# Two-layer decoder trunk, one core: probabilities of pairs 0 to 4 scaled on ScalarE, transposed through DRAM

## The chip, the cores and the metric

The kernel runs on one core of a Trainium2 chip. The metric is the device time of one execution, in microseconds; the figure given is the median of three runs. The core's engines each work through an instruction queue of their own, in order: TensorE (PE; its weight loads are listed as PEld), VectorE (DVE), ScalarE (ACT), GpSimd (POOL) and SyncE (SP), which here only starts transfers.

## The reference

Two decoder layers over 256 tokens of width 1024, 16 heads of 64, float32 throughout. Layer 0 uses forgetting attention: causal softmax, with a bias from the cumulated logarithms of forget gates. Layer 1 uses block-sparse attention, whose one block holds all 256 tokens, so that it is causal softmax with a relative-position bias. Each layer goes on with a gated feed-forward part and a gated embedding.

```python
u = _rmsnorm(h, attn_norm_g[i])
proj = u @ w_in                         # q, k, v (and forget gates in layer 0)
logits = einsum('bhqd,bhkd->bhqk', q, k) * HEAD_DIM ** -0.5 + bias   # -inf above the diagonal
probs = softmax(logits)
o = einsum('bhqk,bhkd->bhqd', probs, v)
h = h + merge_heads(o) @ w_o
u = _rmsnorm(h, ffn_norm_g[i])
gu = u @ ffn_w_in[i]
h = h + (silu(gu[..., :D_FF]) * gu[..., D_FF:]) @ ffn_w_out[i]
gate = sigmoid(_rmsnorm(h, ple_norm_g[i]) @ ple_w_gate[i])
h = h + gate * (p[i] @ ple_w_up[i])
```

At the end stands a last `_rmsnorm`.

## The kernel before

Activations lie with features on the 128 partitions and the 256 tokens along the free axis. Weights stream in chunks of 512 KB on SP's queue into `raw` (six buffers). ScalarE rounds each chunk to the reduced type fp32r (`whi`, L163 and L181), VectorE takes the remainder (`wlo`, L165 and L182), six buffers each, and `mm3` multiplies in three matmuls (L91 to L93): high by high, high by low, low by high. The same split into a high and a low part, `split` (L284 on ScalarE, L285 on VectorE), is made of q and k and of the attention's output.

Attention works on eight pairs of heads (NP = 8). For a pair j:

- `project(j, 0)` and `project(j, 1)`: 48 matmuls into the bank `pq`. VectorE scales the result (`qkt`, L498), then `qkh` and `qkl` are its two parts.
- `scores`: TensorE writes the logits of each head to `sp` (three products L514, and one L511 of the first 128 queries with the first 128 keys; in layer 0 the bias by L371). VectorE adds the mask or bias and takes the extreme of each row (`e`, `mn`, L528; an instruction of 128 columns and one of 256 for each head). ScalarE takes the exponentials and their sums (L532), VectorE the reciprocals of the sums (`rc`, L535), and VectorE multiplies `e` by them (L538, two instructions, for 2 x 128 and 2 x 256 columns).
- `transposes`: six TensorE transposes a pair (L551) put the probabilities' keys on the partitions, in a bank `pp`; ScalarE copies each head's 384 columns out (`pt`, L556).
- `values`: eight instructions of TensorE a pair, with v and `pt`, into `po` (L565 and L567), and a split into the two parts of `o`.

The loop takes two pairs at a time: project pairs j and j+1, then transposes and values of pairs whose probabilities are ready, then the scores of pairs j-1 and j. In its last turn stand the transposes of pairs 3 and 4, values of pairs 1, 2 and 3, the scores of 5 and 6, and those of 7 (their end is `end`). Behind it follow the output weights: `wo(hf, c)` multiplies pairs 2c and 2c+1 into half hf of the output, (0,0) and (1,0) first; between them lie the transposes of pairs 5 to 7 and the values of pairs 4 to 7.

A scheduler sets the order of instructions on each engine from the order in the program; `tc.issue_after(ins)` places what is written inside it behind an instruction. The tiles `e` have four buffers, `pt` four, `fp` four.

At the very end `by_token` turns the output from features to tokens: VectorE transposes blocks of 32 x 32 (L765), two transfers on SP's queue write the result to DRAM (`dh`, L768), and eight read it back in another order (`ut`, L770).

## Time and profile before

| what | value |
|---|---|
| median of three runs | 646.74 us (646.62 to 647.48) |
| profiled execution | 646.52 us |
| its span, first to last instruction | 644.7 us |
| granted TensorE clock | 0.998 |
| TensorE busy | 636.2 us (99%) |
| VectorE busy | 456.0 us (71%) |
| ScalarE busy | 373.7 us (58%) |
| GpSimd busy | 9.9 us (2%) |

All instruction times below are of the profiled execution, counted from the start of its span. The attention of layer 0 lies at about 30 to 105 us, that of layer 1 at 345 to 420 us. A profile row of a group reads: line, engine, operation, output and inputs, shapes and count; then busy time in us and mean of one in ns; then idle time ahead of them and what ended it. A row of a timeline reads: start, duration, engine, line, operation, count, and in brackets idle time ahead of it and what ended it. An arrow names the engine and instruction that was waited for. Neighbouring instructions of one engine overlap by about 0.1 us, so they start at a shorter pitch than their durations.

### The profile page before, as it was taken

The page shows a single profiled execution, that of the slowest core. Times are in us where ns is not written, and L with a number is a line of the kernel's source. Part 1 is how long each engine was busy: PE and PEld are TensorE (multiplying, and loading weights), DVE is VectorE, ACT ScalarE, POOL GpSimd, SP SyncE. Part 2 cuts the span into 40 slices and gives each one's busy share as a digit, 9 for nine tenths or more (in the row PEclk, how much of TensorE's full clock was granted, in tenths as well). Part 3 has the DMA queues.
Part 4 walks back from the last instruction along what each step waited for, and adds up shares of the span by engine and source line. Part 5 has one row for each costly group of instructions (what it writes and reads, how often), then busy time and mean ns, then how long its engine had stood idle before and what let it go on. Part 6 is the DMA issues. An engine that isn't in the chain of part 4 may idle for free.

```text
span 644.7 us, 13185 instructions
## 1 busy us (share of the span) xinstructions
PE 636.2 (99%) x5357; PEld 615.2 (95%) x5357; DVE 456.0 (71%) x734; ACT 373.7 (58%) x633; POOL 9.9 (2%) x23
## 2 busy tenths in 40 slices
PE   9999999999999999999999999999999999999995
PEld 7899999999999999999989999999999999999984
DVE  7789875786666666668895888677666666666685
ACT  6786685754444445448665677666444444454653
POOL 0100000000000000000000000000000000000001
PEclk9999999999999999999999999999999999999999
DMA  8865544397766666666577554436766666666523
GB/s 341 309 207 183 152 132 156 99 348 264 247 199 192 195 192 214 189 205 196 191 245 273 179 173 138 130 102 202 227 199 197 198 197 190 193 205 192 192 97 100
DMA packets 37533, 126.33 MB, mean 196 GB/s; under 512 B 4096, under 2 KB 7776, under 8 KB 37472
## 3 DMA queue, kind: packets, MB, share of 16 engines
q1 hardware_dynamic: 37040, 124.87, 60.7%
q8 instruction: 42, 0.69, 0.4%
q10 hardware_dynamic: 432, 0.62, 0.3%
q14 instruction: 19, 0.16, 0.1%
HBM read 123.35 MB, written 5.27 MB: 200 GB/s over the span
## 4 chain that ended last, share of the span: by engine, by line
PE 96%; issue 2%; DMA 1%; DVE 0%; POOL 0%; POOLq 0%; DVEq 0%; ACT 0%
PE gu L91 12%; PE gu L92 12%; PE gu L93 12%; PE fo L93 6%; PE fo L91 6%; PE fo L92 6%; PE pq L91 5%; PE pq L93 5%; PE pq L92 5%; PE v L422 4%; PE wo L91 2%; PE wo L93 2%; PE wo L92 2%; PE pp L551 2%; PE pg L91 2%
## 5 line engine op out<-in xcount | busy, mean ns | idle before, releaser
L165 DVE TENSOR_TENSOR wlo<-raw,whi 128x1024 fp32r<-128x1024 f32 (+1 forms) x166 | 201.0, 1217 | 84.9 <-ACT whi L163 79.2
L163 ACT ACTIVATE whi<-raw 128x1024 fp32r<-128x1024 f32 x164 | 172.5, 1059 | 120.9 <-issue 53.7
L91 PE MATMUL gu<-g,whi 128*128 128x256 f32 x704 | 194.9, 277 | 0.0
L92 PE MATMUL gu<-g,whi 128*128 128x256 f32 x704 | 194.7, 277 | 0.0
L93 PE MATMUL gu<-g,wlo 128*128 128x256 f32 x704 | 194.5, 276 | 0.0
L93 PEld LDWEIGHTS gu<-g,wlo 128*128 128x128 f32 x704 | 132.2, 188 | 0.0
L92 PEld LDWEIGHTS gu<-g,whi 128*128 128x128 f32 x704 | 132.2, 188 | 0.1
L91 PEld LDWEIGHTS gu<-g,whi 128*128 128x128 f32 x704 | 132.2, 188 | 0.0
L93 PE MATMUL fo<-fp,wlo 128*128 128x256 f32 x352 | 97.4, 277 | 0.0
L91 PE MATMUL fo<-fp,whi 128*128 128x256 f32 x352 | 97.3, 276 | 0.0
L92 PE MATMUL fo<-fp,whi 128*128 128x256 f32 x352 | 97.3, 276 | 0.0
L182 DVE TENSOR_TENSOR wlo<-raw,whi 128x1080 fp32r<-128x1080 f32 x44 | 56.4, 1282 | 41.9 <-ACT whi L181 41.3
L91 PE MATMUL pq<-g,whi 128*128 128x256 f32 x256 | 71.3, 279 | 0.0
L181 ACT ACTIVATE whi<-raw 128x1080 fp32r<-128x1080 f32 x44 | 48.5, 1103 | 38.9 <-PE gu L92 27.1
L93 PE MATMUL pq<-g,wlo 128*128 128x256 f32 x256 | 70.8, 277 | 0.0
L92 PE MATMUL pq<-g,whi 128*128 128x256 f32 x256 | 70.8, 276 | 0.0
L92 PEld LDWEIGHTS fo<-fp,whi 128*128 128x128 f32 x352 | 66.2, 188 | 0.0
L91 PEld LDWEIGHTS fo<-fp,whi 128*128 128x128 f32 x352 | 66.1, 188 | 0.0
L93 PEld LDWEIGHTS fo<-fp,wlo 128*128 128x128 f32 x352 | 66.1, 188 | 0.0
L91 PEld LDWEIGHTS pq<-g,whi 128*128 128x128 f32 x256 | 48.1, 188 | 0.6 <-issue 0.2
L92 PEld LDWEIGHTS pq<-g,whi 128*128 128x128 f32 x256 | 48.1, 188 | 0.1
L93 PEld LDWEIGHTS pq<-g,wlo 128*128 128x128 f32 x256 | 48.1, 188 | 0.0
(184 smaller groups left out, 983.1 us busy)
## 6 DMA issues: line engine op xcount, KB each, us to landing
raw<-w SPq DMA_DIRECT2D x169, 512.0 KB, 4.2
raw<-w SPq DMA_DIRECT2D x44, 540.0 KB, 4.4
d<-d SPq DMA_DIRECT2D x4, 768.0 KB, 7.1
bias<-d SPq DMA_DIRECT2D x4, 512.0 KB, 7.0
dh<-end SPq DMA_DIRECT2D x2, 512.0 KB, 2.6
ut<-dh SPq DMA_DIRECT2D x8, 128.0 KB, 3.0
hw<-wx SPq DMA_DIRECT2D x1, 640.0 KB, 6.5
hw<-xr SPq DMA_DIRECT2D x1, 640.0 KB, 7.8
```

What stands on the lines that cost most here:

```text
L91: mm(o, ah, bh, start=start, stop=False, skip_group_check=True)
L92: mm(o, ah, bl, start=False, stop=False, skip_group_check=True)
L93: return mm(o, al, bh, start=False, stop=stop, skip_group_check=True)
L163: state["hi"] = state[f"hi{i}"] = nc.scalar.activation(hi[:, c], raw[:, c], AF.Copy)
L165: nc.vector.tensor_tensor(lo[:, c], raw[:, c], f32(hi[:, c]), op=ALU.subtract)
L181: nc.scalar.activation(ht, raw[:, 0:WW], AF.Copy)
L182: nc.vector.tensor_tensor(lt, raw[:, 0:WW], f32(ht), op=ALU.subtract)
L422: got = mm(bks[2 * t + hf], x[a][:, t * P:(t + 1) * P], w[b][:, hf * HC:(hf + 1) * HC], start=k + a + b == 0, stop=k + b == KT, skip_group ...
L551: got = nc.tensor.transpose(pp[:, q * P:(q + 1) * P], e[:, s, q * P:(q + 1) * P], ident)
```

## The change

For pairs 0 to 4 of both layers (TURNED = 5):

- VectorE's two multiplies are replaced by four copies on ScalarE with the reciprocal as scale (a head and a part of its columns each).
- The six TensorE transposes and ScalarE's two copies are replaced by `turn`: VectorE transposes the blocks of 32 x 32 in place in two instructions of 128 x 384 (one a head) into a tile `turn` that shares `e`'s four buffers; GpSimd's queue writes it to DRAM in one transfer (`dt`, 128 x 768, 393 KB) and reads it back in four (`pt`, 98 KB each), which put the blocks where the transposed matrix has them. The queue of pending turns is emptied behind the next `qkl`.
- `pt` has two buffers of a pair each, in place of four of a head. `values` reads them as rows of 32 elements, for all pairs.
- The last turn of the loop has no transposes and the values of pairs 1 and 2; those of 3 and 4 stand behind the transposes of pair 5, ahead of `wo(0, 1)`. Layer 1's loop has the same order as layer 0's.

The diff, cut to its core:

```diff
+TURNED = 5
...
 
             th = work.tile([P, 3 * P], F32R, tag="qkh", bufs=3, name=f"qkh{layer}_{j}")
             tl = work.tile([P, 3 * P], F32R, tag="qkl", bufs=3, name=f"qkl{layer}_{j}")
-            split(th, tl, t.rearrange("p a s -> p (a s)")[:, P:])
+            low = split(th, tl, t.rearrange("p a s -> p (a s)")[:, P:])
             qk[j] = t, th, tl
+            with tc.issue_after(low.ins):
+                while fresh:
+                    turn(*fresh.pop(0))
 
         def scores(*js):
 
@@ -535,11 +539,36 @@
                 nc.vector.reciprocal(rc, mn[:, 1])
                 for q in range(2):
                     at = e[:, :, sl[q]]
-                    nc.vector.tensor_tensor(at, at, rc[:, :, q:q + 1].to_broadcast(list(at.shape)), op=ALU.mult)
-                sm[j] = e
+                    if j >= TURNED:
+                        nc.vector.tensor_tensor(at, at, rc[:, :, q:q + 1].to_broadcast(list(at.shape)), op=ALU.mult)
+                        continue
+                    for s in range(2):
+                        nc.scalar.activation(at[:, s], at[:, s], AF.Copy, scale=rc[:, s, q:q + 1])
+                if j < TURNED:
+                    fresh.append((j, e))
+                else:
+                    sm[j] = e
             return got
 
         pts = {}
+
+        fresh = []
+
+        def turn(j, e):
+
+            t = work.tile([P, 4, 3, 2, 32], F32, tag="e", bufs=4, name=f"turn{layer}_{j}")
+            for s in range(2):
+                nc.vector.transpose(t[:, :, :, s].rearrange("p c b x -> p b c x"),
+                                    e[:, s].rearrange("p (b c x) -> p b c x", b=3, x=32))
+            d = dram.tile([P, 6 * P], F32, name=f"dt{layer}_{j}")
+            nc.gpsimd.dma_start(d, t.rearrange("p c b s x -> p (c b s x)"))
+            p = work.tile([P, 4, 3, 2, 32], F32, tag="pt", bufs=2, name=f"pt{layer}_{j}")
+            for i in range(4):
+                nc.gpsimd.dma_start(p[32 * i:32 * i + 32].rearrange("p c b s x -> p c (b s x)"),
+                                    bass.AP(tensor=d.tensor, offset=d.offset + 192 * i,
+                                            ap=[[6 * P, 32], [32 * 6 * P, 4], [1, 192]]))
+            for s in range(2):
+                pts[2 * j + s] = p[:, :, :, s].rearrange("p c b x -> p b c x")
 
         def transposes(j, tag="pt"):
 
@@ -550,10 +579,13 @@
                 for q in range(3):
                     got = nc.tensor.transpose(pp[:, q * P:(q + 1) * P], e[:, s, q * P:(q + 1) * P], ident)
                 if tag == "pt":
-                    pts[i] = work.tile([P, 3 * P], F32, tag="pt", bufs=4, name=f"pt{layer}_{i}")
+                    if s == 0:
+                        both = work.tile([P, 2, 3 * P], F32, tag="pt", bufs=2, name=f"pt{layer}_{j}")
+                    t = both[:, s]
                 else:
-                    pts[i] = work.tile([P, 2 * S], F32, tag="fp", bufs=4, name=f"pt{layer}_{i}")[:, 0:3 * P]
-                nc.scalar.activation(pts[i], pp[:, 0:3 * P], AF.Copy)
+                    t = work.tile([P, 2 * S], F32, tag="fp", bufs=4, name=f"pt{layer}_{i}")[:, 0:3 * P]
+                nc.scalar.activation(t, pp[:, 0:3 * P], AF.Copy)
+                pts[i] = t.rearrange("p (b c x) -> p b c x", b=3, x=32)
             return got
 
         def values(*js):
@@ -562,37 +594,23 @@
             heads = [(slice(s * DH, (s + 1) * DH), slice((2 * j + s) * DH, (2 * j + s + 1) * DH), pts.pop(2 * j + s), po)
                      for j, po in zip(js, pos) for s in range(2)]
             for d, c, t, po in heads:
-                mm(po[d, :S], v[:, 0, c], t[:, 0:S], start=True, stop=False, skip_group_check=True)
+                mm(po[d, :S], v[:, 0, c], t[:, 0:2], start=True, stop=False, skip_group_check=True)
             for d, c, t, po in heads:
-                got = mm(po[d, P:S], v[:, 1, c], t[:, S:], start=False, stop=True, skip_group_check=True)
+                got = mm(po[d, P:S], v[:, 1, c], t[:, 2], start=False, stop=True, skip_group_check=True)
             for j, po in zip(js, pos):
                 split(oh[:, j], ol[:, j], po[:, :S])
             return got
 
 
-        homes = ("pt", "fp") if layer else ("fp", "pt")
         for j in range(0, NP, 2):
             for i in (j, j + 1):
                 project(i, 0)
                 project(i, 1)
+            if j >= 4:
+                values(*range(max(j - 5, 0), j - 3))
+            got = scores(*range(max(j - 1, 0), min(j + 1, NP - 1)))
             if j == NP - 2:
-                for i in (NP - 5, NP - 4):
-                    transposes(i, homes[0])
-                values(NP - 7, NP - 6)
-                values(NP - 5)
-                scores(NP - 3, NP - 2)
                 end = scores(NP - 1)
-            else:
-                turned = layer == 1 and j == 4
-                if turned:
-                    for i in range(j - 3, j - 1):
-                        transposes(i, "fp")
-                if j >= 4:
-                    values(*range(max(j - 5, 0), j - 3))
-                got = scores(*range(max(j - 1, 0), j + 1))
-                if j >= 2 and not turned:
-                    for i in range(max(j - 3, 0), j - 1):
-                        transposes(i)
             if layer == 0 and j == 0:
                 with tc.issue_after(got.ins):
                     moba.extend(moba_bias())
@@ -609,10 +627,11 @@
                     wo(*a)
 
         behind(end, (0, 0), (1, 0))
-        behind(transposes(NP - 3, homes[1]), (0, 1))
-        transposes(NP - 2, homes[1])
-        behind(transposes(NP - 1, homes[0]), (1, 1))
-        values(NP - 4, NP - 3)
+        transposes(NP - 3, "fp")
+        behind(values(3, 4), (0, 1))
+        transposes(NP - 2, "fp")
+        behind(transposes(NP - 1), (1, 1))
+        values(NP - 3)
         behind(values(NP - 2, NP - 1), (0, 2), (1, 2), (0, 3))
         for hf in range(2):
             if hf:
```

VectorE, layer 0, from the reciprocal of pair 3 (`rc_3`) to `qkl` of pair 7. In names like `qkl_7_1062` the first number is the pair, the last one a running number; `wlo` are weights. Before:

```order
L538 TENSOR_TENSOR e_3_879<-e_3_879,rc_3_889 128x2x256
L535 RECIPROCAL rc_4_903<-mn_4_894 128x4
L538 TENSOR_TENSOR e_4_893<-e_4_893,rc_4_903 128x2x128
L538 TENSOR_TENSOR e_4_893<-e_4_893,rc_4_903 128x2x256
L182 TENSOR_TENSOR wlo_1266<-raw_1264,whi_1265 128x1080
L498 TENSOR_TENSOR qkt_6_992<-pq_6_937,row_326 128x512
L182 TENSOR_TENSOR wlo_1320<-raw_1318,whi_1319 128x1080
L285 TENSOR_TENSOR qkl_6_995<-qkt_6_992,qkh_6_994 128x384
L182 TENSOR_TENSOR wlo_1378<-raw_1376,whi_1377 128x1080
L498 TENSOR_TENSOR qkt_7_1059<-pq_7_1004,row_326 128x512
L165 TENSOR_TENSOR wlo_1408<-raw_1406,whi_1407 128x1024
L285 TENSOR_TENSOR qkl_7_1062<-qkt_7_1059,qkh_7_1061 128x384
```

After, the same place (lines moved by one):

```order
L539 RECIPROCAL rc_4_929<-mn_4_920 128x4
L499 TENSOR_TENSOR qkt_6_996<-pq_6_941,row_326 128x512
L183 TENSOR_TENSOR wlo_1273<-raw_1271,whi_1272 128x1080
L286 TENSOR_TENSOR qkl_6_999<-qkt_6_996,qkh_6_998 128x384
L561 STREAM_TRANSPOSE turn_3_1002<-e_3_903 128x3x4x32 x2
L561 STREAM_TRANSPOSE turn_4_1012<-e_4_919 128x3x4x32 x2
L183 TENSOR_TENSOR wlo_1326<-raw_1324,whi_1325 128x1080
L183 TENSOR_TENSOR wlo_1377<-raw_1375,whi_1376 128x1080
L499 TENSOR_TENSOR qkt_7_1083<-pq_7_1028,row_326 128x512
L286 TENSOR_TENSOR o_369<-po_1_1089,o_369 128x256
L286 TENSOR_TENSOR o_369<-po_2_1090,o_369 128x256
L286 TENSOR_TENSOR qkl_7_1086<-qkt_7_1083,qkh_7_1085 128x384
```

The multiplies of pairs 3 and 4 (`e`) are gone; four transposing instructions stand behind `qkl_6`, with two weights and then `qkt_7`, and the remainders of `o` for pairs 1 and 2 stand ahead of `qkl_7`.

ScalarE, layer 0, from the last exponentials of pair 4 to `qkh` of pair 6. Before:

```order
L532 ACTIVATE e_4_893,mn_4_894<-e_4_893,mn_4_894 128x128
L532 ACTIVATE e_4_893,mn_4_894<-e_4_893,mn_4_894 128x256
L556 ACTIVATE pt_2_911<-pp_2_907 128x384
L556 ACTIVATE pt_3_917<-pp_3_913 128x384
L556 ACTIVATE pt_4_923<-pp_4_919 128x384
L556 ACTIVATE pt_5_929<-pp_5_925 128x384
L181 ACTIVATE whi_1265<-raw_1264 128x1080
L181 ACTIVATE whi_1319<-raw_1318 128x1080
L284 ACTIVATE qkh_6_994<-qkt_6_992 128x384
```

After:

```order
L536 ACTIVATE e_4_919,mn_4_920<-e_4_919,mn_4_920 128x256
L546 ACTIVATE e_3_903<-e_3_903,rc_3_913 128x128 x2
L546 ACTIVATE e_3_903<-e_3_903,rc_3_913 128x256 x2
L536 ACTIVATE e_4_919,mn_4_920<-e_4_919,mn_4_920 128x128
L536 ACTIVATE e_4_919,mn_4_920<-e_4_919,mn_4_920 128x256
L182 ACTIVATE whi_1272<-raw_1271 128x1080
L546 ACTIVATE e_4_919<-e_4_919,rc_4_929 128x128 x2
L546 ACTIVATE e_4_919<-e_4_919,rc_4_929 128x256 x2
L285 ACTIVATE qkh_6_998<-qkt_6_996 128x384
```

The four copies of transposed probabilities (`pt`) are gone; the scaling of pair 3 stands between the exponentials of pair 4, and that of pair 4 behind the next weight, ahead of `qkh_6`.

TensorE, layer 0, where the second step of the output weights ends. Before:

```order
L93 MATMUL wo_1_1_1191<-o_369,wlo_1224 128x256
L551 MATMUL pp_10_1252<-con,e_5_1134 128x128 x3
L551 MATMUL pp_11_1258<-con,e_5_1134 128x128 x3
L91 MATMUL wo_0_0_1188<-o_369,whi_1265 128x256
L92 MATMUL wo_0_0_1188<-o_369,whi_1265 128x256
```

After:

```order
L94 MATMUL wo_1_1_1184<-o_369,wlo_1217 128x256
L580 MATMUL pp_10_1245<-con,e_5_1127 128x128 x3
L580 MATMUL pp_11_1251<-con,e_5_1127 128x128 x3
L597 MATMUL po_3_1257<-pt_3_1007,v 64x256 x2
L597 MATMUL po_4_1258<-pt_4_1017,v 64x256 x2
L599 MATMUL po_3_1257<-pt_3_1007,v 64x128 x2
L599 MATMUL po_4_1258<-pt_4_1017,v 64x128 x2
L92 MATMUL wo_0_0_1181<-o_369,whi_1272 128x256
L93 MATMUL wo_0_0_1181<-o_369,whi_1272 128x256
```

The values of pairs 3 and 4 have come between the transposes of pair 5 (`pp_10`, `pp_11`) and `wo(0, 1)`.

GpSimd's queue, layer 0, pairs 1 to 4; before there was nothing between the copy for the forget gates and the next norm's column:

```order
L564 DMA dt_1_788<-turn_1_785 128x768
L564 DMA dt_2_798<-turn_2_795 128x768
L567 DMA pt_1_790<-dt_1_788 32x4x192 x4
L567 DMA pt_2_800<-dt_2_798 32x4x192 x4
L564 DMA dt_3_1005<-turn_3_1002 128x768
L564 DMA dt_4_1015<-turn_4_1012 128x768
L567 DMA pt_3_1007<-dt_3_1005 32x4x192 x4
L567 DMA pt_4_1017<-dt_4_1015 32x4x192 x4
L243 TENSOR_TENSOR col_1633<-ms_1631,nhalf 128x2
```

Each pair's transfers stand in pairs as its turns do: both writes, then the eight reads of the two pairs; behind them comes the column of the norm after the attention.

## The prediction

> **What bounds the kernel now.** I began with the page: busy time by engine, then the chain of work that ended last.

> ```profile
> PE 636.2 (99%) x5357; PEld 615.2 (95%) x5357; DVE 456.0 (71%) x734; ACT 373.7 (58%) x633; POOL 9.9 (2%) x23
> PE 96%; issue 2%; DMA 1%; DVE 0%; POOL 0%; POOLq 0%; DVEq 0%; ACT 0%
> ```

> TensorE (PE) is busy almost all the time and 96% of the chain is PE work, so a microsecond taken from PE is a microsecond gained, as long as no other engine makes PE wait in its place. What the others could make it wait for has to be read in the two attention stages, so the windows come next (busy time and count of PE, PEld, DVE, ACT, POOL; granted clock; DMA share; GB/s).

> ```profile
> 30.00:105.00 75.00, 75.00 (x705) 71.69 (x705) 59.81 (x140) 54.35 (x128) 0.29 (x1) 1.00 0.54 166
> 345.00:420.00 75.00, 75.00 (x699) 72.06 (x698) 55.78 (x133) 50.87 (x121) 0.00 (x0) 1.00 0.52 159
> ```

> Here PE never rests, VectorE (DVE) is busy 80% and 74% of the time against 71% over the whole span, and ScalarE (ACT) 72% and 68%. DVE has only some 15 us of free time in 75, and what counts is where these lie. So I read the timelines of PE and DVE around the last two pairs (start, duration, instruction).

> ```profile
> 54.03 0.88 PE L551 MATMUL pp<-con,e 128*128 128x128 f32 x6
> 54.66 0.36 PE L91 MATMUL pq<-g,whi 128*128 128x256 f32 x1
> ...
> 80.59 1.47 PE L551 MATMUL pp<-con,e 128*128 128x128 f32 x12
> 81.99 1.08 PE L565 MATMUL po<-pt,v 128*64 128x256 f32 x8
> ...
> 83.34 0.60 PE L565 MATMUL po<-pt,v 128*64 128x256 f32 x4
> ...
> 84.09 0.71 PE L511 MATMUL sp<-qkt 64*128 64x128 f32 x8
> ...
> 85.70 0.39 PE L511 MATMUL sp<-qkt 64*128 64x128 f32 x4
> ...
> 86.55 0.39 PE L91 MATMUL wo<-o,whi 128*128 128x256 f32 x1
> ...
> 92.13 0.82 PE L551 MATMUL pp<-con,e 128*128 128x128 f32 x6
> ```

> Before, PE works through: the last projection ends at 80.59, 12 transposes (1.40 to the next start), values of two pairs (1.35), of one pair (0.75 with the step to the scores), scores of pairs 5 and 6 (1.61), of pair 7 (0.85), and the output weights from 86.55.

> ```profile
> 63.69 0.55 DVE L285 TENSOR_TENSOR qkl<-qkt,qkh 128x384 fp32r<-128x384 f32 x1
> ...
> 68.82 0.28 DVE L528 CUSTOM_DVE_ANT_0 e<-sp,con 128x128 f32<-128x128 f32 x1
> ...
> 71.04 0.18 DVE L535 RECIPROCAL rc<-mn 128x4 f32<-128x4 f32 x1
> 71.25 1.03 DVE L538 TENSOR_TENSOR e<-e,rc 128x256 f32<-128x256 f32 x2
> 72.80 0.18 DVE L535 RECIPROCAL rc<-mn 128x4 f32<-128x4 f32 x1 [0.52 <-ACT e L532]
> ...
> 75.29 1.28 DVE L182 TENSOR_TENSOR wlo<-raw,whi 128x1080 fp32r<-128x1080 f32 x1 [1.25 <-ACT whi L181]
> 76.49 0.68 DVE L498 TENSOR_TENSOR qkt<-pq,row 128x512 f32<-128x512 f32 x1
> 77.09 1.28 DVE L182 TENSOR_TENSOR wlo<-raw,whi 128x1080 fp32r<-128x1080 f32 x1
> 78.28 0.55 DVE L285 TENSOR_TENSOR qkl<-qkt,qkh 128x384 fp32r<-128x384 f32 x1
> ...
> 80.79 0.69 DVE L498 TENSOR_TENSOR qkt<-pq,row 128x512 f32<-128x512 f32 x1 [0.37 <-PE pq L93]
> ...
> 82.95 0.55 DVE L285 TENSOR_TENSOR qkl<-qkt,qkh 128x384 fp32r<-128x384 f32 x1
> ...
> 85.72 0.29 DVE L528 CUSTOM_DVE_ANT_0 e<-sp,con 128x128 f32<-128x128 f32 x1 [0.62 <-PE sp L371]
> ...
> 94.23 1.22 DVE L165 TENSOR_TENSOR wlo<-raw,whi 128x1024 fp32r<-128x1024 f32 x1
> ```

> DVE waits behind both reciprocals' exps and at 75.29, that is, just where the removed multiplies stand. At qkt of pair 7 (80.79) it waits only for PE, and qkl of pair 7 begins 2.75 us ahead of pair 7's scores.

> **The change part by part.** *Transposes taken from PE.* Six of them cost 0.63 us, twelve 1.40. Per layer go 6, 12 and 12, so 3.43, in both layers **6.9 us**. That is all the change can gain on PE. The reads of values in runs of 32 elements have no row; between no cost and as much again as they take now (1.35 for two pairs, so 6.8 for ten) I take none, by the nearest rows that read an operand in pieces, DVE's: the multiply over two strided heads (685 ns, below) costs no more than a turn of as many contiguous columns (687). The upper end is in the range with half its size.

> *Multiplies taken from DVE, scaling given to ACT.* DVE loses 0.94 us a pair (1.03, less the overlap of neighbours). ACT loses two copies and gains four scaled ones a pair.

> ```profile
> L556 ACT ACTIVATE pt<-pp 128x384 f32<-128x384 f32 x32 | 13.2, 482 | 0.4 <-PE pp L551 0.4
> 72.67 1.59 ACT L556 ACTIVATE pt<-pp 128x384 f32<-128x384 f32 x4
> L201 ACT ACTIVATE g<-h,gx 128x256 fp32r<-128x256 f32 x40 | 18.2, 500 | 5.2 <-DVE h L317 2.8 <-DVE h L320 1.6 <-DVE h L740 0.4
> L532 ACT ACTIVATE e<-e,mn 128x128 f32<-128x128 f32 x32 | 12.5, 392 | 8.9 <-DVE mn L528 8.9
> ```

> Four copies take 1.59 us where 4 x 482 ns make 1.93: each hides 0.09 behind its neighbour. The scaled copies are like L201 (scale by a column, 500 ns for 256 columns) and for 128 columns like the exp's 392 ns: 2 x 0.50 + 2 x 0.39, less 4 x 0.09, is 1.42 a pair, 0.6 more than the copies were. What matters is its place: the scaling of pair 3 stands ahead of the last two exps of pair 4, so the reciprocal of pair 4 comes 1.42 later than its exps would let it, and the scaling of pair 4 and a weight's rounding stand ahead of qkh of pair 6. The DVE time saved is thus time in which DVE waits for ACT.

> *Turns given to DVE.* Two STREAM_TRANSPOSE of 128x384 a pair.

> ```profile
> L538 DVE TENSOR_TENSOR e<-e,rc 128x512 f32<-128x512 f32 x16 | 11.0, 685 | 0.0
> L765 DVE STREAM_TRANSPOSE end<-h 128x512 f32<-128x512 f32 x4 | 2.6, 687 | 0.0
> L285 DVE TENSOR_TENSOR qkl<-qkt,qkh 128x384 fp32r<-128x384 f32 x16 | 8.8, 551 | 0.0
> ```

> 687 ns for 512 columns, the multiply's 685 for as many, so for 384 columns the 551 of qkl, or 0.47 in a row: 0.94 a pair, 1.88 for two pairs in the place where qkl of pair 6 releases DVE to qkt of pair 7.

> *DVE walked through layer 0* (pitches 0.60 for qkt, 0.47 for qkl, 0.34 for a value's remainder, 1.14 and 1.20 for weights of 1024 and 1080 columns). qkl of pair 4 at 63.51, turns to 65.86, two weights 68.20, qkt of pair 5 68.80, a remainder and a weight 70.28, qkl 70.75: there e of pair 3 begins, 1.93 after 68.82. The reciprocal of pair 4 is 1.93 + 1.42 later, at 76.15, and qkt of pair 6 at 76.3 is no later than before: the multiplies and the 1.25 of idle have gone into it. From there the lag shows. ACT does a rounding and the scaling of pair 4 first, so qkl of pair 6 begins at 78.94; ends 79.4, turns to 81.3, two weights to 83.7 of which one stood elsewhere before, and only then qkt of pair 7, though its projection ends at 78.6 (80.59 less 0.63 and 1.35). With two remainders between, qkl of pair 7 ends at 85.5. Pair 7's scores could start at 78.6 + 1.35 + 1.61 = 81.6 and end at 82.4; but a part of them, taken as 0.6 of their 0.85, needs qkl, so the output weights start at 86.1: **0.4 us earlier than before instead of 4.1**.

> *The tail.* Values of pairs 3 and 4 now stand between the first two and the third step of the output weights: one pair more than before after 86 us, +0.65. Their remainder on DVE stands behind the weight that before began at 94.23. DVE enters this stretch at 86.65 and not 85.72, so that weight ends at 95.4 + 0.93 and the remainder at 96.7. PE wants it at 86.1 + 5.58 (two steps, 86.55 to 92.13) + 0.63 (six transposes) + 1.35 (values) + 1.4 (half a step) = 95.05: +1.65. Layer 0: -0.4 + 0.65 + 1.65 = **+1.9**.

> *Layer 1*, walked in the same way from these rows:

> ```profile
> 388.43 0.18 DVE L535 RECIPROCAL rc<-mn 128x4 f32<-128x4 f32 x1 [0.52 <-ACT e L532]
> 395.24 1.47 PE L551 MATMUL pp<-con,e 128*128 128x128 f32 x12
> 400.69 0.38 PE L91 MATMUL wo<-o,whi 128*128 128x256 f32 x1
> 407.60 0.85 ACT L556 ACTIVATE pt<-pp 128x384 f32<-128x384 f32 x2
> ```

> Here DVE reaches e of pair 3 almost on time (a wait for PE takes up the turns of pairs 1 and 2), so the reciprocal of pair 4 comes at 388.43 + 0.1 + 1.42 = 389.95. Behind it: qkt to 390.7, the scaling and a rounding on ACT, qkl of pair 6 at 392.74 to 393.2, turns to 395.1, a weight to 396.3, qkt of pair 7 to 396.9, a weight, and qkl to 398.65. The projection ends at 395.24 - 0.63 - 1.40 = 393.2. The output weights start at 399.05 (0.4 for what of the scores needs qkl, which has no forget bias here): 1.65 earlier and not 4. The remainder of pair 3 follows a weight whose rounding stands behind the two copies of 407.60, and ends at 410.4; PE wants it at 408.0. -1.65 + 0.65 + 2.4 = **+1.4**. In pairs 0 to 2 of both layers the lag ends in DVE's waits for PE, so I take nothing there. The rounded weights have six buffers, at 2.8 us a step (half of 5.58) some 16 us of lead, which covers shifts of up to 3 us.

> *GpSimd's transfers*, 50 in all, one out and four back a pair; the only other thing in that queue, the norm's column after the attention, is far later. SP's queue keeps its order. e of pair 7 waits for the buffer of pair 3's turn, free when its write has landed (82.95, worked out below), well ahead of 85.7. The nearest rows are the kernel's last ones, the same turn through DRAM on SP.

> ```profile
> dh<-end SPq DMA_DIRECT2D x2, 512.0 KB, 2.6
> ut<-dh SPq DMA_DIRECT2D x8, 128.0 KB, 3.0
> 625.40 3.68 SPq L770 DMA_DIRECT2D ut<-dh  x8
> ```

> Pair 3's turn ends at about 80.35, lands at 82.95; then eight loads of c each, the last landing 3.0 after issue. PE wants pair 4's at 93.0, and until 94.6 the late remainder hides it. So c may be 1.08 us. From below, SP issued eight in 3.68, c = 0.46: pair 4 is there at 89.6, cost nothing. From above, each waits for the one before to land: 24 us, at 107, 12 us a layer. I take nothing, from the row of eight loads on one queue, the nearest in kind; layer 1 has the same allowance.

> [...] No row before shows a transfer of GpSimd. [...]

> **Sum.** +1.9 and +1.4 are +3.3; the profiled execution took 646.52 (span 644.7, 1.8 outside), which is 0.2 under the median of 646.74. Prediction 649.8.

> **Rivals.** *All of it hidden* (faster): DVE keeps up, since its average load has room. For it speaks 15 us of free DVE time in 75; against it, that this lies ahead of the reciprocals. 6.9 less nothing: 639.9. Halfway, with no stall for the remainder of pair 3 but the late qkl, layer 0 has +0.25 and layer 1 -1.0: 646. With what the stalls cost (3.3 + 6.9 = 10.2) halved, 644.7.
> *Transfers late* (slower still): past c = 1.08, each 0.1 us costs 0.8 us a layer. At c = 1.5 it is 3.4 a layer: 656.5. One by one, 12 a layer: 674.
> *Turning point.* The change is faster if qkl of pair 7 is done by about 83.5 in layer 0 and 396.5 in layer 1, with the remainder of pair 3 in time.

> **How the numbers follow.** A measurement tells about 0.2% from nothing, here 1.3 us: 645.4 to 648.0. My case with errors of 2 us either way, 648.0 to 652: 0.43. Transfers late, above 652: 0.18. Stalls partly there, 643 to 648: 0.27, of which 0.11 is below 645.4. All hidden: 0.12. Faster is 0.23, same 0.16, slower 0.61. The range leaves out the fully hidden case and transfers slower than c = 1.5: 643.0 to 657.0.

> **What would show it.** After: no L551 in pairs 0 to 4; DVE rows with long waits "<-ACT e" at both reciprocals; qkt of pair 7 at about 83.7, with PE idle 3 us ahead of pair 7's scores; a wait of 2 us in the output weights on DVE's remainder of pair 3; GpSimd's loads landed before PE asks. I am wrong if the scheduler's order lets DVE catch up, if a turn or scaled copy costs other than 0.47 and 0.36, or if values wait for a GpSimd transfer.

## The result, and the profile after

The changed kernel takes 652.11 us (median of four runs, 651.87 to 653.96) against 646.89 for the kernel before (four runs): ratio of the means 1.0086, interval 1.0066 to 1.0105. It is slower, by 5.2 us; the forecast was 649.8. The profiled execution took 652.11, with a span of 650.3 against 644.7 (+5.6) and a mean granted clock of 0.997 against 0.998.

From the page after: busy time by engine, and the chain of work that ended last.

```profile
PE 634.3 (98%) x5297; PEld 611.4 (94%) x5297; DVE 453.7 (70%) x734; ACT 378.4 (58%) x653; POOL 37.8 (6%) x73
PE 79%; ACT 8%; DVE 7%; issue 4%; POOL 0%; POOLq 0%; DVEq 0%; DMA 0%; ACTq 0%
```

PE lost 60 instructions, but only 1.9 us of busy time, and its share of the chain fell from 96% to 79%: ACT and DVE now stand in it. Where they do is seen in the two attention stages (windows; columns as before).

```profile
30.00:105.00 75.00, 71.22 (x653) 66.77 (x651) 57.16 (x137) 56.35 (x136) 14.24 (x26) 1.00 0.68 211
345.00:420.00 75.00, 71.48 (x638) 67.53 (x638) 53.85 (x132) 54.14 (x131) 13.78 (x25) 1.00 0.68 219
```

PE was busy all 75 us of both, and now stands still for 3.8 and 3.5. DVE is busy *less* than before (57.16 against 59.81, 53.85 against 55.78), although PE now waits for it. The list of PE's waits (us in total, times, longest) names them:

```profile
PE po L597 <- DVE rc L539: 3.4, 2, 1.8
PE sp L515 <- DVE qkt L499: 2.0, 2, 1.4
PE sp L518 <- DVE qkl L286: 0.9, 2, 0.7
PE po L597 <- DVE e L543: 0.8, 2, 0.5
```

Together 7.1 us, where the same list of the kernel before has nothing but the cold start (0.8) and a wait of 0.2. The first and last lines are to be read with care: `po` multiplies `pt`, and the reciprocal and the multiply named belong to pair 7 (in layer 0 they end at 93.79 and 94.85), whose probabilities these values do not use. It is the transfer of `pt` that came last: in the trace the last reads of pairs 3 and 4 land at 93.77 and 94.82, and the values start at 93.91 and 95.01. Two experiments below have the same wait under the name "DMA pt<-dt", and without transfers it is gone (`e1_no_transfer`).

PE and DVE around the last pairs of layer 0 (timelines; the idle time ahead of a row is in brackets), for the same places as in the prediction:

```profile
79.49 1.08 PE L597 MATMUL po<-pt,v 128*64 128x256 f32 x8
...
84.13 0.49 PE L515 MATMUL sp<-qkt 64*128 64x128 f32 x4 [1.41 <-DVE qkt L499]
...
85.28 0.38 PE L518 MATMUL sp<-qkl,qkh 64*128 64x256 f32 x2 [0.21 <-DVE qkl L286]
...
85.88 0.38 PE L92 MATMUL wo<-o,whi 128*128 128x256 f32 x1
...
93.91 0.65 PE L597 MATMUL po<-pt,v 128*64 128x256 f32 x4 [1.65 <-DVE rc L539]
...
95.01 0.65 PE L597 MATMUL po<-pt,v 128*64 128x256 f32 x4 [0.45 <-DVE e L543]
```

```profile
75.89 0.18 DVE L539 RECIPROCAL rc<-mn 128x4 f32<-128x4 f32 x1 [2.96 <-ACT e L536]
75.99 0.66 DVE L499 TENSOR_TENSOR qkt<-pq,row 128x512 f32<-128x512 f32 x1
...
78.69 0.56 DVE L286 TENSOR_TENSOR qkl<-qkt,qkh 128x384 fp32r<-128x384 f32 x1 [0.52 <-ACT qkh L285]
79.16 1.95 DVE L561 STREAM_TRANSPOSE turn<-e 128x384 f32<-128x384 f32 x4
...
83.39 0.69 DVE L499 TENSOR_TENSOR qkt<-pq,row 128x512 f32<-128x512 f32 x1
...
84.66 0.56 DVE L286 TENSOR_TENSOR qkl<-qkt,qkh 128x384 fp32r<-128x384 f32 x1
```

The values of pairs 1 and 2 begin at 79.49 instead of 81.99, 2.5 us earlier, straight behind the last projection, which before ended at 80.59 with twelve transposes behind it. But `qkt` of pair 7 comes at 83.39 instead of 80.79, so the output weights begin only 0.67 earlier (85.88 against 86.55). The tail then gives that back: PE waits 1.65 and 0.45 us for transfers. GpSimd's timeline, for both transfers of pairs 3 and 4:

```profile
80.49 0.56 POOL L564 DMA_DIRECT2D dt<-turn  x1 [5.98 <-DVE turn L561]
81.41 0.56 POOL L564 DMA_DIRECT2D dt<-turn  x1 [0.36 <-DVE turn L561]
85.76 4.37 POOL L567 DMA_DIRECT2D pt<-dt  x8 [3.79 <-DMA dt<-turn]
```

And the list of transfers, with count, size and median us from issue to landing:

```profile
dt<-turn POOLq DMA_DIRECT2D x10, 384.0 KB, 4.0
pt<-dt POOLq DMA_DIRECT2D x40, 96.0 KB, 5.5
```

Pair 3's write is issued at 80.49 and lands, by the trace, at 85.16; the reads, which wait for it, begin at 85.76, 5.3 us behind its issue. The eight reads issue 0.55 us apart (4.37 / 8), and a read takes 5.5 us to land (median).

### The profile page after: what moved, and what is told of

It reads as the page before. It is cut to its first block, busy times and chain, and to the rows that moved or that the text cites. A ratio compares the mean times of both kernels' runs of the same rounds, so it can differ in the third digit from the quotient of the medians.

```text
span 650.3 us, 13150 instructions
## 1 busy us (share of the span) xinstructions
PE 634.3 (98%) x5297; PEld 611.4 (94%) x5297; DVE 453.7 (70%) x734; ACT 378.4 (58%) x653; POOL 37.8 (6%) x73
## 4 chain that ended last, share of the span: by engine, by line
PE 79%; ACT 8%; DVE 7%; issue 4%; POOL 0%; POOLq 0%; DVEq 0%; DMA 0%; ACTq 0%
PE gu L92 12%; PE gu L93 12%; PE gu L94 12%; PE fo L94 6%; PE fo L93 6%; PE fo L92 6%; ACT e L536 4%; PE v L423 3%; DVE wlo L166 2%; PE wo L92 2%; PE wo L93 2%; PE wo L94 2%; ACT e L546 2%; PE pg L92 1%; PE pg L93 1%
## 5 line engine op out<-in xcount | busy, mean ns | idle before, releaser
L93 PE MATMUL gu<-g,whi 128*128 128x256 f32 x704 | 194.7, 277 | 0.0
L93 PEld LDWEIGHTS gu<-g,whi 128*128 128x128 f32 x704 | 132.2, 188 | 0.0
L93 PE MATMUL fo<-fp,whi 128*128 128x256 f32 x352 | 97.3, 276 | 0.0
L93 PE MATMUL pq<-g,whi 128*128 128x256 f32 x256 | 71.0, 278 | 0.0
L182 ACT ACTIVATE whi<-raw 128x1080 fp32r<-128x1080 f32 x44 | 48.3, 1101 | 38.7 <-PE gu L93 27.1
L93 PEld LDWEIGHTS fo<-fp,whi 128*128 128x128 f32 x352 | 66.2, 188 | 0.0
L93 PEld LDWEIGHTS pq<-g,whi 128*128 128x128 f32 x256 | 48.2, 188 | 0.1
## 6 DMA issues: line engine op xcount, KB each, us to landing
raw<-w SPq DMA_DIRECT2D x169, 512.0 KB, 3.7
bias<-d SPq DMA_DIRECT2D x4, 512.0 KB, 7.6
dh<-end SPq DMA_DIRECT2D x2, 512.0 KB, 2.6
ut<-dh SPq DMA_DIRECT2D x8, 128.0 KB, 2.9
```

The source lines that it names most:

```text
L93: mm(o, ah, bl, start=False, stop=False, skip_group_check=True)
L182: nc.scalar.activation(ht, raw[:, 0:WW], AF.Copy)
```

## The experiments

Each stands against runs of the kernel before on the same chip; the ratio is to these, with its interval.

**Is it the transfers?** `e1_no_transfer`: the turns write straight into the tiles that `values` reads. It leaves out the moving of the blocks, so its values are those of probabilities that are transposed only within blocks; the transposes of pairs 5 and 7 swap their tiles to make room.

```diff
-            t = work.tile([P, 4, 3, 2, 32], F32, tag="e", ...)
+            # pairs 2 and 3: two tiles "fp"; pairs 0, 1, 4: one tile "pt"
...
-            nc.gpsimd.dma_start(d, ...)
-            for i in range(4): nc.gpsimd.dma_start(p[32 * i:32 * i + 32], ...)
```

> The changed kernel without the way through DRAM: VectorE's transposing instructions write straight into the tiles that the values read (so the 32 x 32 blocks stay where they were and the values are computed from them), and all 50 transfers of GpSimd are gone. Theory A (two chains end together at the third step of the output weights, GpSimd's transfers at 95.0 us and VectorE's remainder of pair 3 behind its weights at 96.7): the 2.1 us waits ahead of the values of pairs 3 and 4 go, but a wait for the remainder of pair 3 appears instead, and only 0.6 to 0.8 us a layer is gained: 650.3 to 651.0. Rival B (the transfers alone set that place): 2.1 us a layer, 647.9. In both, qkt of pair 7 stays late (about 83.4 us) and the 2.5 us around pair 7's scores stay.

650.68 us, 1.006 (1.0045 to 1.0075). With no transfer at all only some 1.4 us come back of the 5.2, though PE waited 4.2 us for transfers. In their place comes the wait that the prediction had there, for the remainder of `o` of pair 3 (waits of PE; the 0.9 is in layer 0, while in layer 1 this execution ran 3.4 us at half clock, the granted clock 0.63 from 402 to 404 us and 0.51 from 404 to 406, and PE came later):

```profile
PE wo L93 <- DVE o L286: 0.9, 1, 0.9
```

So the late transfers stood in front of a wait for DVE that was there anyway. Part of what the transfers are worth is hidden by the clock: in the 3.4 us at half clock (the missing share of the two windows, doubled) a matmul of 256 columns starts every 0.21 us and behind them every 0.11 to 0.12 us, so they cost up to 1.7 us by my estimate, and all four executions have a mean granted clock of 0.993 or 0.994, where those of the change have 0.994 to 0.997. The same from the other side, `e7_sp_queue`: the change, with its transfers on SP's queue.

```diff
-            nc.gpsimd.dma_start(d, ...)
+            nc.sync.dma_start(d, ...)
-                nc.gpsimd.dma_start(p[32 * i:32 * i + 32], ...)
+                nc.sync.dma_start(p[32 * i:32 * i + 32], ...)
```

> The changed kernel with its 50 transfers issued by SP in place of GpSimd, among the weights. Theory A (the transfers' part in the loss is how late GpSimd's land: writes 4.0 and reads 5.5 us where I had counted 2.6 and 3.0 from SP's rows): reads of pair 4 are there at about 90 us, the waits ahead of the values of pairs 3 and 4 go, and the time is that without transfers (e1, 650.7): 650.2 to 651.2. Rival B (the landing is slow because the weights' traffic shares the 16 DMA engines, whoever issues): 652.1 as the change, or 1 to 3 us more where SP's waiting for a turn holds weights back.

650.28 us, 1.0053 (1.0038 to 1.0068). The list of its transfers:

```profile
dt<-turn SPq DMA_DIRECT2D x10, 384.0 KB, 4.1
pt<-dt SPq DMA_DIRECT2D x40, 96.0 KB, 3.1
```

The reads land in 3.1 us, near the 3.0 that I had taken from the kernel's last transfers; in the change, on GpSimd's queue, they took 5.5. The write takes 4.1 here and 4.0 there. PE waits for no values any more, but in layer 1 for both parts of pair 3's `o` (waits of PE; in layer 0 this execution ran 3.4 us at half clock, a matmul every 0.21 us from 86.6 to 90.0 us and every 0.11 to 0.12 us ahead of it and behind, and PE came later):

```profile
PE wo L93 <- DVE o L286: 0.9, 1, 0.9
PE wo L92 <- ACT o L285: 0.5, 1, 0.5
```

The gain is 1.8 us. Queue and transfers are thus worth 1.4 to 1.8 us as measured, and somewhat more where the half clock hides a part.

**Is it ScalarE's scaling?** `e2_dve_scale`: the multiplies go back to VectorE; turns and transfers stay.

```diff
-                    if j >= TURNED:
+                    if True:
                         nc.vector.tensor_tensor(at, at, rc[...], op=ALU.mult)
```

> The changed kernel with VectorE's two multiplies a pair put back for pairs 0 to 4 in place of ScalarE's four scaled copies; turns and transfers as in the change. If VectorE's removed multiplies stood in its waits for ScalarE (my theory), giving them back costs nothing and taking ScalarE's 1.42 us a pair out of the way makes qkt of pair 7 earlier: about 82.6 instead of 83.4 in layer 0, the whole 0.5 to 0.9 us a layer faster, 650.3 to 651.1. If VectorE's busy time is what counts (rival), 0.94 us for each of two pairs comes on top: 1.9 us a layer slower, 655.9.

647.59 us, 1.001 (1.0001 to 1.002): 4.5 us faster than the change, far more than I expected, and nearly as fast as the kernel before. The opposite, `e8_scale_only`: the kernel before with nothing but the scaling of pairs 0 to 4 given to ScalarE.

```diff
+                    if j >= 5:
                         nc.vector.tensor_tensor(at, at, rc[...], op=ALU.mult)
+                        continue
+                    for s in range(2):
+                        nc.scalar.activation(at[:, s], at[:, s], AF.Copy, scale=rc[:, s, q:q + 1])
```

> One part of the change alone: the kernel before with pairs 0 to 4 scaled by ScalarE's four copies in place of VectorE's two multiplies; transposes, copies, order of the values as before. ScalarE then has 1.42 us a pair more ahead of qkh of pair 6. Theory (ScalarE's place in the chain exps, scaling, qkh is what hurt): qkt and qkl of pair 7 come 1 to 2 us later than before and part of it reaches TensorE: 0.5 to 2 us a layer slower, 648 to 651. Rival (VectorE's lag from the turns is needed for it to hurt): 646.8.

650.00 us, 1.0049 (1.0032 to 1.0066). The scaling alone makes the kernel 3.1 us slower, with PE's transposes where they were. Where it begins is seen in one group, the reciprocals, of four kernels (busy, mean ns, then the idle time of DVE ahead of them): before, after, `e2_dve_scale`, `e8_scale_only`.

```profile
L535 DVE RECIPROCAL rc<-mn 128x4 f32<-128x4 f32 x16 | 2.8, 176 | 3.3 <-ACT e L532 3.1
```

```profile
L539 DVE RECIPROCAL rc<-mn 128x4 f32<-128x4 f32 x16 | 2.8, 176 | 11.9 <-ACT e L536 11.8
```

```profile
L539 DVE RECIPROCAL rc<-mn 128x4 f32<-128x4 f32 x16 | 2.8, 176 | 3.3 <-ACT e L536 3.1
```

```profile
L535 DVE RECIPROCAL rc<-mn 128x4 f32<-128x4 f32 x16 | 2.8, 176 | 13.1 <-ACT e L532 12.9
```

Wherever ScalarE scales, DVE stands 8.6 to 9.8 us longer at the reciprocals. The multiplies taken from it were 9.4 us (ten pairs of 0.94). DVE works less and is no earlier; what was behind it in its queue (`qkt`, turns, remainders) gained nothing. PE's waits in `e8_scale_only`:

```profile
PE pp L555 <- DVE o L285: 0.7, 1, 0.7
PE po L569 <- ACT pt L560: 0.6, 2, 0.3
```

These are 1.3 us only. By the marks of the trace three places hold 3.0 of the 3.2 us by which its profiled execution is longer, the waits among them: the twelve transposes of pairs 1 and 2 in layer 0 (2.54 us to the next step, before 1.35), and the values of pairs 1 to 3 in both layers (2.97 and 3.01, before 2.10). At the values PE waits for ScalarE's copies `pt`, and ScalarE itself had waited 1.1 us for VectorE's late `qkt`. The rest of the 3.0 counts as busy time of PE.

PE's waits in `e2_dve_scale`:

```profile
PE po L597 <- DMA pt<-dt: 1.1, 2, 0.8
PE sp L518 <- DVE qkl L286: 0.9, 2, 0.6
...
PE sp L515 <- DVE qkt L499: 0.6, 1, 0.6
```

2.6 us against 7.1 after the change: 4.5 fewer, as much as the medians differ by. That the two agree so well is partly chance: this profiled execution is one of its longer ones (648.58, with 3.4 us at half clock; windows in the last section) and 3.5 us shorter than the change's. The waits for values shrink too. In layer 0 pair 3's write is issued 1.0 us earlier (79.47), its reads begin 0.3 us later (86.03), but they land sooner, on the same queue:

```profile
pt<-dt POOLq DMA_DIRECT2D x40, 96.0 KB, 3.2
```

So the 5.5 us of the change are not a property of GpSimd's queue alone; what else makes a read slow there was not tested.

**Is it the place of the turns?** `e4_turn_late`: the turns of pairs 3 and 4 no longer stand behind `qkl` of pair 6, but behind that of pair 7.

```diff
-                while fresh:
+                while fresh and j != NP - 2:
```

> The changed kernel with the turns of pairs 3 and 4 placed behind qkl of pair 7 instead of pair 6. qkl of pair 7 is then done at about 84.2 instead of 85.2 us in layer 0 and the output weights start 1.0 to 1.5 us earlier, but the writes to DRAM start about 4.2 us later (84.7 instead of 80.5). Theory A (the transfers now end last ahead of the third step): the values of pairs 3 and 4 end about 4 us later, so 3.4 to 4.2 us a layer slower, 659 to 660. Rival B (VectorE's lag ahead of pair 7 is all that counts and the transfers have room): 1.0 to 1.5 us a layer faster, 649.5.

663.93 us, 1.0254 (1.0234 to 1.0274). The scores of pair 7 start sooner, and the output weights wait for all that comes later: 3.2 us on the remainders, 3.0 on a transfer.

```profile
PE wo L92 <- DVE o L286: 3.2, 2, 1.7
PE po L597 <- DMA pt<-dt: 3.0, 1, 3.0
```

These are waits of up to 3 us. PE was busy for 1.83 of the 4 us from 84 us on and for 1.11 of those from 96 us on, and in the windows right behind the granted clock was 0.57 and 0.50 (columns as before):

```profile
88.00:92.00 4.00, 4.00 (x24) 4.00 (x23) 3.51 (x21) 4.00 (x18) 1.50 (x3) 0.57 0.44 168
100.00:104.00 4.00, 4.00 (x22) 3.67 (x19) 0.42 (x1) 0.38 (x1) 0.00 (x0) 0.50 0.07 26
```

So the place that the change gives the turns is the better of the two. The half clock can have cost up to 9.2 us, enough for the loss beyond my 659 to 660; I have not separated it. (That is an estimate from the mean granted clocks of the two profiled executions, 0.983 here and 0.997 after the change: 0.014 of a span of 660.1 us.) Even without all of that the profiled execution (661.89) would be no faster than the change.

**Fewer pairs.** `e3_turned3`: only pairs 0 to 2 go the new way; the last turn of the loop and the tail are as before, except that the transposes of pairs 3 and 4 stand behind the values of 1 and 2, and the values of pair 3 between the scores of 6 and 7.

```diff
-TURNED = 5
+TURNED = 3
...
+            if j == NP - 2:
+                for i in (3, 4):
+                    transposes(i, homes[0])
             got = scores(*range(max(j - 1, 0), min(j + 1, NP - 1)))
             if j == NP - 2:
+                values(3)
                 end = scores(NP - 1)
```

> The change for pairs 0 to 2 alone (TURNED = 3): pairs 3 and 4 keep VectorE's multiplies, TensorE's transposes and ScalarE's copies as before; values of pairs 1 and 2 at their place, transposes of 3 and 4 ahead of the scores of 5 and 6, values of 3 between these and the scores of 7, values of 4 with those of 5. Then no turn stands ahead of qkt of pair 7 and no transfer ahead of the output weights. Theory: TensorE loses 18 transposes a layer, 2.0 us, and waits nowhere: 4.0 us under before, 643, less up to 1 us a layer for VectorE's lag from the turns of pairs 1 and 2. Rival (the loss comes from any turn or any transfer, or from TensorE's matmul pitch, which was 118 ns instead of 113.5 for projections 4 to 7 of the changed kernel's layer 0): 646 to 648.

646.31 us, 0.9991 (0.9982 to 1.0001): no difference from the kernel before that can be told, and 3 us more than I expected. PE's waits are all but gone (0.4 us for one transfer). Part of what spoilt it is seen in the pace of back-to-back matmuls. The projections are 96 matmuls between the first `pq` row and the next `po` row. The kernel before needs 11.08 us for those of pairs 4 and 5, that is 115 ns each (54.66 above, and this row):

```profile
65.74 0.65 PE L565 MATMUL po<-pt,v 128*64 128x256 f32 x4
```

After the change, and in `e3_turned3` too, the same 96 take 11.50 us, 120 ns each (the rows are those of the change):

```profile
53.97 0.38 PE L92 MATMUL pq<-g,whi 128*128 128x256 f32 x1
...
65.47 0.65 PE L597 MATMUL po<-pt,v 128*64 128x256 f32 x4
```

The granted clock is 1.00 before and after the change (windows from 30 to 105 us). So there is a faster and a slower pace: between 54 and 65.4 us the median from one matmul's start to the next is 113 ns before and 118 after. That the pace is set where PE starts anew behind other work was my guess, which no run settled. The kernel before has a layout that may bear on it: `gapped()`, which lays a weight chunk with 56 empty columns behind its first block, used for the first chunk behind some of the breaks.

The pace is not all. In `e3_turned3` the projections of pairs 4 to 7 take 1.1 us longer than before (0.9 of it in layer 0, by the pace). Another 1.8 us lie between the last projection and the output weights, where its order differs from before: 6.66 and 6.55 us in the two layers, before 5.96 and 5.45, with the wait of 0.4 among them. That is 2.9 of the 4.0 us of transposes saved; the start of this execution happened to be 0.9 us longer besides.

**The pace.** `e5_kick`: multiplies on VectorE as in `e2_dve_scale`, and three more gapped chunks: in layer 0 the second of pairs 4 and 6 beside the first, and `wo(1, 2)`.

```diff
-            elif j > 2 and (...) and a == 0 or layer and j == 4:
+            elif j > 2 and (...) and a == 0 or layer and j == 4 or not layer and j in (4, 6):
                 hi, lo = gapped()
...
-KICK = ((0, 0), (0, 1), (1, 1), (0, 2))
+KICK = ((0, 0), (0, 1), (1, 1), (0, 2), (1, 2))
```

> The kernel of e2 (VectorE scales, all else as in the change) with the gapped layout of a weight chunk, which the kernel uses at some chunks, at three more: the second chunk of projections 4 and 6 of layer 0, and the output weights' step (1, 2) of both layers. In every kernel with turns, matmuls of 256 columns followed each other at 118 ns instead of 113.5 from 54 to 80 us, and in those with five pairs turned also for 14 to 22 us from about 103 and 416 us; before had 113.5 there. Theory: which of the two paces runs on is set at a break and by the layout of the first chunk behind it, so the changed order ahead of these places lost the fast pace; a second gap gets it back, as in layer 1 of before, where pace 118 at 369.8 us ended with the next gapped chunk at 372.6. Then about 1.5 to 2.0 us faster than e2 (647.6): 645.6 to 646.1. Rival: the pace has another cause (the transfers, the strided reads of the values): unchanged, 647.6.

647.92 us, 1.0012 (1.0003 to 1.0021): not different from `e2_dve_scale`. The slow stretches did get shorter in the trace (behind 55 us it lasts for one chunk, 2.8 us), but PE then waits more at the values (1.0 us for a transfer, and 0.4 behind it for which the profile names no event, against 1.1 in `e2_dve_scale`). I read it so: a faster PE only came to the same transfers earlier.

`e6_three_kick` puts three things together: the order of `e3_turned3`, multiplies on VectorE, and the two more gapped chunks in layer 0's projections.

```diff
-TURNED = 5
+TURNED = 3
-                    if j >= TURNED:
+                    if True:
-            elif j > 2 and (...) and a == 0 or layer and j == 4:
+            elif j > 2 and (...) and a == 0 or layer and j == 4 or not layer and j in (4, 6):
                 hi, lo = gapped()
```

> The kernel of e3 (turns of pairs 0 to 2 alone) with VectorE's multiplies for all pairs and the gapped layout at the second chunk of projections 4 and 6 of layer 0. Theory: e3 (646.3) lost 0.9 us of its 4.0 to the slow pace of 54 to 80 us, of which 0.7 come back, and 0.3 to ScalarE's scaling: 645.0 to 645.4, 0.2 to 0.3% under before. Rival (pace not set by the layout, scaling of three pairs hidden): 646.3.

645.02 us, 0.9973 (0.9963 to 0.9983): faster than the kernel before, by 1.8 us. In its windows PE stands still nowhere in the attention, and the 96 matmuls take 11.21 us (windows, then two rows of PE's timeline):

```profile
30.00:105.00 75.00, 75.00 (x697) 71.18 (x696) 61.76 (x146) 53.14 (x122) 8.73 (x16) 1.00 0.62 198
345.00:420.00 75.00, 75.00 (x693) 71.60 (x692) 59.00 (x140) 48.10 (x114) 8.28 (x15) 1.00 0.59 188
```

```profile
53.85 0.38 PE L92 MATMUL pq<-g,whi 128*128 128x256 f32 x1
...
65.06 0.65 PE L597 MATMUL po<-pt,v 128*64 128x256 f32 x4
```

DVE is busy longer than in the change (61.76 against 57.16), and nobody waits for it.

`e9_three_plain`: the same with no gapped chunk in the projections of pairs 4 to 7 of layer 0.

```diff
-            elif j > 2 and (...) and a == 0 or layer and j == 4 or not layer and j in (4, 6):
+            elif layer and (j in (4, 6) and a == 0 or j == 5 and a == 0 or j == 4):
```

> The kernel of e6 with no gapped chunk at all in projections 4 to 7 of layer 0 (e6 has them at both chunks of projections 4 and 6, e3 at the first). In e6 the first, gapped chunk behind the scores ran at 118 ns and the second, gapped again, at 113.5. Theory (the first chunk's layout sets the pace after a break; it was fitted to a break that ends in transposes, which the change removes): with a plain first chunk the matmuls run at 113.5 ns from 54 us on, all four projections, and the kernel is 0.3 to 0.5 us faster than e6 (645.0): 644.5 to 644.7. Rival (behind scores the pace is 118 until a gap resets it): slow through 54 to 79 us, 0.5 us slower than e6: 645.5.

645.02 us, 0.9973 (0.9963 to 0.9984). The projections of pairs 4 and 5 ran fast (11.09 us), as the theory had it, but the first two steps of the output weights ran slow in their place (85.0 to 90.7 us: 5.77 us, against 5.58 in `e6_three_kick`). The total is the same; what sets the pace is not settled.

`e10_five_best` is `e5_kick` with the transfers on SP's queue, to see whether five pairs can match three.

```diff
-            nc.gpsimd.dma_start(d, ...)
+            nc.sync.dma_start(d, ...)
-                nc.gpsimd.dma_start(p[32 * i:32 * i + 32], ...)
+                nc.sync.dma_start(p[32 * i:32 * i + 32], ...)
```

> All five pairs with what the runs so far favour: VectorE's multiplies for all pairs, transfers issued by SP, and the three more gapped chunks of e5. Theory: of e5's 647.9, waits of 1.4 us for transfers go, and those for qkt and qkl of pair 7 (1.9) stay: 646.0 to 646.8, so five pairs do not beat three (645.0) since the turns of pairs 3 and 4 still stand ahead of qkt of pair 7. Rival (transfers were the last thing that five pairs lost to): 644.5 or less.

646.31 us, 0.9997 (0.9988 to 1.0006): as the kernel before, and 1.3 us behind `e6_three_kick`. PE still waits 1.9 us for `qkt` and `qkl` of pair 7, as expected, and 0.5 for a remainder of `o`. `e11_kick_wo` is the change with `wo(1, 2)` gapped and nothing else.

```diff
-KICK = ((0, 0), (0, 1), (1, 1), (0, 2))
+KICK = ((0, 0), (0, 1), (1, 1), (0, 2), (1, 2))
```

> The changed kernel itself with one more gapped chunk, at the output weights' step (1, 2) of both layers, the second step behind the last values. From 105.3 to 127.2 us and from 419.1 to 434.3 us its matmuls followed each other at 118 ns; between the first matmul of step (0, 2) and the first scores of layer 1 it lost 0.75 us to before, and 0.6 us behind layer 1's attention. Theory (these 1.35 us are the pace): the gap ends the slow stretch of layer 0 after one step, as it did in e5 at 103.5 us, and perhaps that of layer 1, where e5 ended one and got another: 0.7 to 1.2 us faster, 650.9 to 651.4. Rival (the 1.35 us are weights that arrive late, or the transfers): unchanged, 652.1.

651.89 us, 1.0081 (1.0066 to 1.0096), not to be told from the change. In the trace the stretch from `wo(0, 2)` to layer 1's first scores is 253.36 us long, against 254.01 after the change and 253.26 before: the slow pace there was 0.75 us, and the chunk takes back 0.65. Its profiled execution has a half-clock stretch near 400 us that the change's has not: the granted clock from 400 to 405 us is 0.66, after the change 1.00.

## Why the prediction was right, and where not

The forecast was 649.8, slower; the time is 652.11, at the edge between its main case (648.0 to 652) and "transfers late". The sum by its own stretches, from the same marks in both traces (first scores of pairs 1 and 2 in layer 0, first `wo`, `wo(0, 2)`, first scores of layer 1, its first `wo`, its last values, end):

| stretch | forecast | before, us | after, us | measured |
|---|---|---|---|---|
| to the first scores of pairs 1 and 2 | 0 | 52.32 | 52.27 | -0.05 |
| layer 0, to the output weights | -0.4 | 34.23 | 33.61 | -0.62 |
| layer 0, the tail, to `wo(0, 2)` | +2.3 | 15.86 | 19.23 | +3.37 |
| rest of layer 0 | 0 | 253.26 | 254.01 | +0.75 |
| layer 1, to the output weights | -1.65 | 45.02 | 43.25 | -1.77 |
| layer 1, the tail | +3.05 | 15.52 | 18.82 | +3.30 |
| behind it | 0 | 228.5 | 229.1 | +0.6 |
| sum | +3.3 | 644.7 | 650.3 | +5.6 |

*Transposes taken from PE, turns, scaled copies.* The durations were right. So was taking nothing for the reads of values in runs of 32 elements: the values of three pairs take 2.10 us in both traces (81.99 to 84.09 before, 103.01 to 105.11 after). Forecast: a turn 551 ns, scaled copies 500 and 392. The groups after:

```profile
L561 DVE STREAM_TRANSPOSE turn<-e 128x384 f32<-128x384 f32 x20 | 9.9, 547 | 0.0
L546 ACT ACTIVATE e<-e,rc 128x256 f32<-128x256 f32 x20 | 8.9, 494 | 0.0
L546 ACT ACTIVATE e<-e,rc 128x128 f32<-128x128 f32 x20 | 6.8, 387 | 0.0
```

*DVE's saved time is time in which it waits for ACT.* Shown, by the group of reciprocals in four kernels and by `e8_scale_only`.

*DVE walked through layer 0.* It held to 0.35 us: `rc` of pair 4 at 76.15 forecast, 75.89 measured; `qkt` of pair 6 76.3, 75.99; `qkl` of pair 6 78.94, 78.69; `qkt` of pair 7 83.7, 83.39; the output weights 86.1, 85.88. In layer 1 they came at 402.37, of which 3.45 is layer 0's shift: 398.92, forecast 399.05. The projection's end did not hold (78.6 forecast, 79.49 measured, the slow pace), but PE waited for DVE there, so it cost nothing. PE's idle time ahead of and in pair 7's scores was 1.6 us in the rows (1.41 and 0.21), not the 3 us named as a sign.

*The tail.* Here a step failed, in both layers: I took nothing for GpSimd's transfers, with landings of 2.6 and 3.0 us from SP's rows, and let only their issue c be unknown. c was 0.55, near its lower end of 0.46 and far from the 1.08 at which I saw a cost. But the landings were 4.0 and 5.5. The wait of 2 us for pair 3's remainder, named as a sign, did not come, and a sign of being wrong did: values waited for a GpSimd transfer. The rival "transfers late" came true in its effect, for a reason that its condition did not name: PE waited 1.65 and 0.45 us for values in layer 0 (above), and in layer 1

```profile
410.51 0.65 PE L597 MATMUL po<-pt,v 128*64 128x256 f32 x4 [1.76 <-DVE rc L539]
...
411.73 0.65 PE L597 MATMUL po<-pt,v 128*64 128x256 f32 x4 [0.36 <-DVE e L543]
```

That is 4.2 us. The waits forecast there, for pair 3's remainder, were 1.65 and 2.4, that is 4.05, and did not show at all, since PE came later. Without late transfers they do, but smaller: 0.94 in layer 0 (`e1_no_transfer`) and 0.5 + 0.9 in layer 1 (`e7_sp_queue`), 2.4 in all. Each is read in the layer that had no half clock in that execution. So two terms were mis-sized and cancel, which is luck: the remainder by 1.65 too much, the transfers by 1.8 too little (4.2 less 2.4; `e1_no_transfer` and `e7_sp_queue` gained 1.4 and 1.8).

*Not in the sum.* What makes the time 2.3 us longer than forecast is in none of its waits. Of the tails' +3.37 and +3.30, the waits for values are 2.1 each and the moved pair 0.65; 0.6 and 0.5 are left, in which PE was busy. 0.75 and 0.6 came in the rest of layer 0 and behind layer 1's attention, where the change touches nothing. Together 2.45. For the 0.75 it is shown to be the matmuls' pace: from 105 to 127 us PE starts a matmul every 118 ns (median), the kernel before every 113, at a granted clock of 1.00 in both, and `e11_kick_wo`, with another layout of one chunk, took 0.65 of it away. The stretch is 254.01 us long after the change, in `e1_no_transfer`, `e2_dve_scale` and `e7_sp_queue`, which turn five pairs without that layout, and 253.26 to 253.27 before and in the four that turn three or none. Of the 0.6, 0.3 lies in the first 20 us, with the same slow pace (419 to 434 us: 118 ns, before 113); the other 0.3 lies behind PE's last matmul, a stretch that is 7.2 to 8.2 us long in the thirteen profiled executions whatever the kernel, so it is noise. For the tails' 1.1 I have no experiment.

*"Halfway" and "all of it hidden"* did not come: DVE did not catch up. With the multiplies left on DVE and fewer turns ahead of pair 7 it does, and there the change's gain appears (`e6_three_kick`), though small. In its profiled execution the attention ends 2.58 us earlier than before (last values of layer 1 at 413.63 against 416.21), while 36 of the 60 transposes, by the prediction's 6.9 us some 4.1, are gone. What is missing is in PE's busy time, so it is no wait. The trace places it: the projections of pairs 4 to 7 take 0.5 us longer than before in the two layers, most of it by the pace, and the stretches between the last projection and the output weights 1.4 longer (6.52 and 6.25 us against 5.96 and 5.45), where the values of pair 3 now stand between the scores. Why these take longer is not shown. (The start and layer 1's tail were 0.4 us shorter, so that only some 1.5 of the 1.9 show.) Another 0.7 lies behind PE's last matmul, in the stretch that varies by as much from one execution to the next.

## What to carry to other kernels

Work moved from one in-order engine to another frees nothing if the first then waits for the second at the very next instruction (here VectorE lost 9.4 us of multiplies and stood 8.6 us longer at the reciprocals): look at what stands behind the moved work on *both* queues before counting its busy time as saved. Price a transfer by a range of landings, and not by one like transfer on another queue at another place: the same reads landed in 3.2 and 5.5 us (medians) on the same queue, in two kernels that differ only in who scales. When PE waits for two late things in a row, removing the later one is worth only the difference; here 4.2 us of waits for transfers were worth 1.4 to 1.8.
